# Softmax row maxima taken as minima of scaled scores inside the score pass

## The chip, the core and the metric

The kernel runs on one core of a Trainium2 chip. Its time is the device time of one execution in microseconds (us); the profile shows one execution engine by engine: PE (TensorE matmuls), PEld (its weight loads), DVE (VectorE), ACT (ScalarE), POOL (GpSimd) and SP (which issues most loads).

## What is computed

One decoder layer over 512 tokens of width 1024, in float32. The part that the change touches is the two softmaxes of the attention stage:

```python
# A: sliding window, 8 heads in 4 blocks of 128 queries; a learned sink per head is one more score
scores = where(valid, q @ k * d**-0.5 - slope * delta, -1e30)
probs = softmax(concat([scores, sink]))[..., :-1]
# B: differential attention, 4 heads with two maps each, 4 blocks of 128 queries
scores = where(delta >= 0, q @ k * d**-0.5 - slope * delta, -1e30)
p = softmax(scores)
a = p[:, :, 0] - lam * p[:, :, 1]
```

Around them stand an adaLN-modulated norm, one input projection, gates with their own projections, a merge, an output projection, a second norm, a gated MLP with a width-3 convolution, and a final norm. `slope` is a power of two: 2^-(h+1) for the 8 heads of A, 2^-(2h+2) for the 4 heads of B.

## The kernel before, in words

Every product in float32 accuracy is made of three matmuls on operands split into a high and a low half (`mm3`, L121). The low halves are computed on DVE (L119, L491, L494), the high halves on ACT (L118, L490, L493).

**Order of the work.** In the attention stage only TensorE's order is written by hand. It consists of attention steps and, between them, of *filling* steps: `fill(n)` (L539) runs n steps of the projections that wait in `units`, each step three matmuls of 512 columns. `SWA_FILL` and `DIFF_FILL` say how many stand at each place. DVE, ACT, POOL and SP get their order when the kernel is built, from priorities (`tc.high_priority(offset=HP)` marks the softmax work), a model of each instruction's time, and explicit holds (`tc.issue_after`). Every eighth fill step also starts a piece of the adaLN row products (`ada_rows`, L839: a weight load, then multiplies of 128x512 on DVE, L857 and L859).

**Sliding-window pairs.** Four pairs i of heads h = i + 4j, j = 0, 1. `swa_scores` (L587) makes the scores of a pair in PSUM and then, for each block n and each j, one score pass on DVE (L620): it adds the distance matrix `dsw` to the scores, writes the sum to `sb`, and leaves the row maximum in `mx[:, j, n]`. In the trace it is a CUSTOM_DVE_ANT_0 and a DVE_READ_ACCUMULATOR2_ANT, the readout of the row value. The scores are kept divided by the slope, so that the distance enters with factor 1. `swa_softmax` (L625) turns the maxima of a head into the exponential's bias (L631: minus slope times maximum, and the minimum of that and `nsink`, which is minus the sink), computes the sink's exponential `es` (L632), four exponentials with row sums (L635, scale `slope`), the sum with the sink (L639), its reciprocal (L640), and the normalisation (L644). Then PE transposes the probabilities (`swa_transpose`, L656), ACT copies them out (L658), and `swa_values` multiplies them by v (L666).

**Differential blocks.** s = 4h + n runs over 4 heads and 4 query blocks. `diff_scores` (L716) and `diff_softmax` (L751) take two blocks together: score passes with row maxima for both maps (L744, with the distance matrix `ddf`), maxima times minus slope (L754), exponentials (L764), and on DVE the weight of the second map (L767, L768) and the difference (L769). `diff_transpose` transposes it (L781) and splits it into `aTh` and `aTl` (L490, L491). `diff_values` (L786) multiplies by v into `od`; its statistics (`stats`, L801) and the normalisation by `turn_norm` (L812: transposes `rb`, L815, then `of` times `rb`, L816, and the split into `outd`, L817 by L118 and L119) come later, for the last head at set numbers of fill steps after it.

**The end of the stage** (L998 to L1004): four gate units are added, four fill steps run, the third head's `turn_norm` is flushed, and `diff_values` of the last head runs; after that the fill steps go on until the units are used up. The merge with the differential branch (`pB`, L1044) reads `outd`.

Of the kernel before, what the change touches and what calls it, by code (L numbers as in the profile page):

```python
# [8 lines left out]
F32 = mybir.dt.float32  # L9
F32R = mybir.dt.float32r  # L10
AF = mybir.ActivationFunctionType
ALU = mybir.AluOpType
PSUM = bass.MemoryType.PSUM

P = 128
# [3 lines left out]
NT = S // P  # L19
# [35 lines left out]
def kernel(  # L55
# [22 lines left out]
    nc = tc.nc  # L78
# [3 lines left out]
    def pool(name, bufs=1, space=None, stack=ctx):  # L82
        kw = {} if space is None else {"space": space}
        return stack.enter_context(tc.tile_pool(name=name, bufs=bufs, reuse_waits="tile", **kw))
# [61 lines left out]
    dsw = cpool.tile([P, 256], F32, name="dsw")  # L146
# [3 lines left out]
    ddf = cpool.tile([P, 512], F32, name="ddf")  # L150
# [290 lines left out]
    for gi in range(KT):  # L441
# [4 lines left out]
        else:  # L446
            h_low(gi)
            lp = cpool.tile([P, 2, 64], F32, name="lp")
            ls = cpool.tile([P, 2], F32, name="ls")
# [4 lines left out]
            nsink = cpool.tile([P, 8], F32, name="nsink")  # L454
# [27 lines left out]
    ap = pool("att", stack=at)  # L482
# [51 lines left out]
    def prefetch():  # L534
        while units and len(loaded) < 2:
            load, run = units.pop(0)
            loaded.append((load(), run))

    def fill(n):  # L539
        for _ in range(n):  # L540
            if not current:
                prefetch()
                if loaded:
                    wts, run = loaded.pop(0)
                    current.append(run(wts))
                    if tick[0]:
                        prefetch()
            if tick[0] == 7:
                prefetch()
            if current:  # L550
                try:
                    next(current[0])
                except StopIteration:
                    current.clear()
            for e in list(later):
                e[0] -= 1
                if e[0] <= 0:
                    later.remove(e)
                    e[1]()
            tick[0] += 1  # L560
            if tick[0] >= ADA_START and tick[0] % ADA_EVERY == 0:
                next(ada, None)
# [24 lines left out]
    def swa_scores(i, blocks):  # L587
        if 0 in blocks:
            c = pairs[i] = Pair()
            c.mx, c.nm, c.lsum, c.es = (  # L590
                ap.tile([P, 2, NT], F32, tag=t, bufs=2, name=f"{t}{i}") for t in ("mx", "nm", "lsum", "es")
            )
            c.sb = [ap.tile([P, 2, P], F32, tag="st0", bufs=2, name=f"st{i}_0")]
            c.sb += [ap.tile([P, 2, 256], F32, tag="st", bufs=ST, name=f"st{i}_{n}") for n in range(1, NT)]
            c.pT = []
        c = pairs[i]
        sps = {
            (g, j): vbank(f"sw{i}_{g}_{j}").rearrange("p (a q) -> p a q", a=2)
            if len(blocks) == NT and (g, j) == (1, 1) else sbank(f"sw{i}_{g}_{j}", (P, 2, 256))
            for g in sorted({n // 2 for n in blocks}) for j in range(2)  # L600
        }
        for n in blocks:
            w = P if n == 0 else 2 * P
            k0 = max(0, n - 1) * P
            qs, ks = slice(n * P, (n + 1) * P), slice(k0, k0 + w)
            mm3_rows([
                (
                    sps[n // 2, j][:, n % 2, :w],
                    [qa[64 * j : 64 * j + 64, i, b, qs] for b in range(2)],
                    [ka[64 * j : 64 * j + 64, b, ks] for b in range(2)],  # L610
                )
                for j in range(2)
            ])
        for n in blocks:
            w = P if n == 0 else 2 * P
            if n == 2:
                c.first = c.last
            for j in range(2):
                with tc.high_priority(offset=HP):
                    c.last = nc.vector.tensor_tensor_reduce(  # L620
                        c.sb[n][:, j, :w], sps[n // 2, j][:, n % 2, :w], dsw[:, 256 - w : 256], 1.0, -3e38, ALU.add, ALU.max,
                        c.mx[:, j, n : n + 1],
                    )

    def swa_softmax(i):  # L625
        with tc.high_priority(offset=HP):
            c = pairs[i]
            for j in range(2):
                h = i + 4 * j
                slope = 2.0 ** -(h + 1)  # L630
                nc.vector.tensor_scalar(c.nm[:, j], c.mx[:, j], -slope, nsink[:, h : h + 1], ALU.mult, ALU.min)  # L631
                nc.scalar.activation(c.es[:, j], c.nm[:, j], AF.Exp, bias=sink[:, h : h + 1])  # L632
                for n in range(NT):
                    w = P if n == 0 else 2 * P
                    nc.scalar.activation(  # L635
                        c.sb[n][:, j, :w], c.sb[n][:, j, :w], AF.Exp, bias=c.nm[:, j, n : n + 1], scale=slope,
                        accum_out=c.lsum[:, j, n : n + 1],
                    )
                nc.vector.tensor_add(c.lsum[:, j], c.lsum[:, j], c.es[:, j])  # L639
                nc.vector.reciprocal(c.lsum[:, j], c.lsum[:, j])  # L640
                for n in range(NT):
                    w = P if n == 0 else 2 * P
                    sb = c.sb[n][:, j, :w]
                    c.divided = nc.vector.tensor_scalar_mul(sb, sb, c.lsum[:, j, n : n + 1])  # L644
# [71 lines left out]
    def diff_scores(*ss):  # L716
        ops = []
        for s in ss:
            h, n = divmod(s, NT)
            t = heads[h]  # L720
            w = (n + 1) * P
            if n == 0:
                firsts[h] = [sbank(f"sd{h}_{m}", (P, 2, 256)) for m in range(2)]
            sps = [
                firsts[h][m][:, n, :w] if n < 2 else (vbank if n + m == 4 else sbank)(f"sd{h}_{n}_{m}")[:, :w]
                for m in range(2)
            ]
            mm3_rows([
                (
                    sps[m],  # L730
                    [t[64 * m : 64 * m + 64, b, n * P : (n + 1) * P] for b in range(2)],
                    [t[64 * m : 64 * m + 64, 2 + b, :w] for b in range(2)],
                )
                for m in range(2)
            ])
            ops.append((s, sps, w))
        for s, sps, w in ops:
            h, n = divmod(s, NT)
            mx = ap.tile([P, 2], F32, tag="dmx", bufs=3, name=f"dmx{h}_{n}")
            pm = []  # L740
            for m in range(2):
                st = ap.tile([P, w], F32, tag="st", bufs=ST, name=f"sd{h}_{n}_{m}")
                with tc.high_priority(offset=HP):
                    nc.vector.tensor_tensor_reduce(  # L744
                        st, sps[m], ddf[:, 512 - w : 512], 1.0, -3e38, ALU.add, ALU.max, mx[:, m : m + 1]
                    )
                pm.append(st)
            scored[s] = mx, pm


    def diff_softmax(*ss):  # L751
        with tc.high_priority(offset=HP):
            for s in ss:
                nc.vector.tensor_scalar_mul(scored[s][0], scored[s][0], -(2.0 ** (-2 * (s // NT + 1))))  # L754
            behind = ExitStack()
            for s in ss:
                h, n = divmod(s, NT)
                slope = 2.0 ** (-2 * (h + 1))
                mx, pm = scored[s]
                if n == 0:  # L760
                    sums[h] = ap.tile([P, 2, NT], F32, tag="dls", bufs=2, name=f"dls{h}")
                ls0, ls1 = (sums[h][:, m, n : n + 1] for m in range(2))
                for m, ls in enumerate((ls0, ls1)):
                    exp = nc.scalar.activation(  # L764
                        pm[m], pm[m], AF.Exp, bias=mx[:, m : m + 1], scale=slope, accum_out=ls
                    )
                nc.vector.reciprocal(ls1, ls1)  # L767
                nc.vector.scalar_tensor_tensor(ls1, ls1, ls0, nlam, ALU.mult, ALU.mult)  # L768
                last = nc.vector.scalar_tensor_tensor(pm[0], pm[1], ls1, pm[0], ALU.mult, ALU.add)  # L769
                probs[s] = pm[0]  # L770
                behind.enter_context(tc.issue_after(exp.ins))
                behind.enter_context(tc.issue_after(last.ins))
            behind.close()
# [144 lines left out]
    pairs, firsts, scored, probs, aTs = {}, {}, {}, {}, {}  # L918
# [49 lines left out]
    for s in range(4 * DIFF_HEADS):  # L968
        h, n = divmod(s, NT)
# [27 lines left out]
            fill(DIFF_FILL[3])  # L997
    for j in range(4, KT):  # L998
        add_gate_a(j)
    fill(4)  # L1000
    flush("norm")
    diff_values(DIFF_HEADS - 1)
    while units or loaded or current:
# [220 lines left out]
    st = gpart(3, [P, 2, 4, 256], "s1_t1")  # L1224
# [716 lines left out]
```

## Time and profile before

| | before |
|---|---|
| median of 3 runs | 693.09 us (692.62 to 693.96) |
| the profiled execution | 693.06 us |
| its span, first to last instruction | 691.3 us |
| mean granted TensorE clock | 0.996 |
| sliding-window score passes (L620) | 59.1 to 100.2 us from the span's start |
| differential score passes (L744) | 114.8 to 195.1 us |
| MLP, up projection (L1270) and down projection (L1885) | from 355 and from 579 us |

In the lines of the profile that follow, times are us from the span's start unless marked ns; `out<-in` names the tiles that an instruction writes and reads, then comes the shape (partitions x elements), and `[0.49 <-DVE st L644]` is idle time of the engine before the instruction and what ended it. Matmuls are pipelined, so their durations overlap and the distance of their starts is what one costs. A row of the waits reads: engine, tile, line, released by whom, us in total, times, longest.

### The profile page before, as it was taken

How to read it: one execution, taken by the hardware profiler on the slowest of the kernel's cores; microseconds unless marked ns; L12 is line 12 of the kernel's file. 1: busy time of each engine (PE TensorE's matmuls, PEld its weight loads, DVE VectorE, ACT ScalarE, POOL GpSimd, SP SyncE). 2: the span in 40 equal slices, each digit the busy share in tenths (PEclk: the TensorE clock that was granted, in tenths of full speed). 3: DMA queues.
4: the chain of work that ended last, by engine and by line, in shares of the span. 5: the costliest groups of instructions: out<-in, count | busy, mean ns of one | idle time of the engine just before them, and what ended most of it. 6: DMA issues, size and time to landing. Idle time of an engine off the chain costs nothing. (4 is left out here: it accounts for less than half of the span.)

```text
span 691.3 us, 11249 instructions
## 1 busy us (share of the span) xinstructions
PE 680.5 (98%) x4203; PEld 592.7 (86%) x4203; DVE 565.3 (82%) x1073; ACT 384.6 (56%) x686; POOL 82.1 (12%) x100
## 2 busy tenths in 40 slices
PE   8999999999999999999999999999999999999995
PEld 5787877788888888888889999999999999888884
DVE  5898987987885666663789988888888999979997
ACT  7676666545552323332477756655565666656665
POOL 3000000000001000000030101112111002540300
PEclk9999999999999999999999999999999999999998
DMA  9985454553455675229726798777978748997903
GB/s 307 328 258 165 140 156 151 154 163 96 138 138 169 212 217 180 91 95 315 230 56 129 166 214 197 167 173 215 206 215 217 155 149 207 196 195 199 167 1 121
DMA packets 115926, 121.81 MB, mean 176 GB/s; under 512 B 4447, under 2 KB 93344, under 8 KB 115872
## 3 DMA queue, kind: packets, MB, share of 16 engines
q1 hardware_dynamic: 96958, 95.09, 43.8%
q0 software_dynamic: 18720, 25.73, 22.2%
q8 instruction: 33, 0.54, 0.3%
q10 hardware_dynamic: 194, 0.28, 0.1%
q14 instruction: 21, 0.17, 0.1%
HBM read 118.97 MB, written 2.11 MB: 175 GB/s over the span
## 5 line engine op out<-in xcount | busy, mean ns | idle before, releaser
L1270 PE MATMUL up<-t,m_whi 128*128 128x256 f32 x512 | 93.1, 283 | 0.0
L1270 PEld LDWEIGHTS up<-t,m_whi 128*128 128x128 f32 x512 | 79.9, 192 | 0.0
L1270 PE MATMUL up<-t,m_wlo 128*128 128x256 f32 x256 | 72.4, 283 | 0.0
L1270 PE MATMUL up<-bh,p_whi 128*128 128x256 f32 x232 | 65.7, 283 | 0.0
L1270 PE MATMUL up<-bl,p_whi 128*128 128x256 f32 x232 | 65.7, 283 | 0.0
L1270 PE MATMUL up<-bh,p_wlo 128*128 128x256 f32 x232 | 65.7, 283 | 0.0
L859 DVE SCALAR_TENSOR_TENSOR arow<-ra,cs,arow 128x512 f32<-128x512 f32 x56 | 42.0, 749 | 20.0 <-DMA ra<-in_w_ada_dram 19.4
L1270 PEld LDWEIGHTS up<-t,m_wlo 128*128 128x128 f32 x256 | 49.2, 192 | 0.0
L1270 PEld LDWEIGHTS up<-bh,p_whi 128*128 128x128 f32 x232 | 44.5, 192 | 0.0
L1270 PEld LDWEIGHTS up<-bl,p_whi 128*128 128x128 f32 x232 | 44.5, 192 | 0.0
L1270 PEld LDWEIGHTS up<-bh,p_wlo 128*128 128x128 f32 x232 | 44.5, 192 | 0.0
L1179 POOL DMA_DIRECT2D s<-in_w_up_dram x21 | 27.0, 1361 | 140.8 <-DMA s<-in_w_up_dram 66.5
L1207 ACT CAST m_whi<-s 128x1024 fp32r<-128x1024 f32 x31 | 32.5, 1049 | 11.1 <-DVE s L1201 6.3
L1211 DVE TENSOR_TENSOR m_wlo<-s,m_whi 128x1024 fp32r<-128x1024 f32 x31 | 37.8, 1219 | 0.0
L1270 PE MATMUL up<-t,p_whi 128*128 128x256 f32 x176 | 32.2, 283 | 0.0
L882 POOL DMA_DIRECT2D mod_rows<-row x8 | 4.9, 614 | 204.9 <-ACT row L881 204.9
L1270 PEld LDWEIGHTS up<-t,p_whi 128*128 128x128 f32 x176 | 27.5, 192 | 0.0
L1277 ACT ACTIVATE gT<-a,cv 128x512 f32<-128x512 f32 x22 | 17.8, 816 | 16.9 <-DVE a L1312 15.8
L185 POOL TENSOR_TENSOR r<-ms,mhalf 128x1 f32<-128x1 f32 (+1 forms) x16 | 12.6, 791 | 120.9 <-DVE ms L183 73.1
L1207 ACT CAST p_whi<-wa 128x1024 fp32r<-128x1024 f32 x18 | 18.8, 1046 | 12.5 <-PE up L1270 12.5
L1211 DVE TENSOR_TENSOR p_wlo<-wa,p_whi 128x1024 fp32r<-128x1024 f32 x18 | 22.0, 1223 | 3.8 <-ACT p_whi L1207 3.8
L1270 PE MATMUL up<-t,p_wlo 128*128 128x256 f32 x88 | 24.9, 283 | 0.0
(491 smaller groups left out, 2064.9 us busy)
## 6 DMA issues: line engine op xcount, KB each, us to landing
ra<-in_w_ada_dram SPq DMA_DIRECT2D x32, 512.0 KB, 4.4
wa<-in_w_up_dram SPq DMA_DIRECT2D x22, 512.0 KB, 3.9
s<-in_w_up_dram SPq DMA_DIRECT2D x21, 512.0 KB, 4.5
s<-in_w_up_dram POOLq DMA_DIRECT2D x21, 512.0 KB, 6.6
adaw<-in_w_ada_dram SPq DMA_DIRECT2D x12, 512.0 KB, 7.6
w<-in_w_in_dram SPq DMA_DIRECT2D x12, 512.0 KB, 4.9
a<-in_w_up_dram SPq DMA_DIRECT2D x11, 512.0 KB, 4.5
b<-in_w_down_dram SPq DMA_DIRECT2D x10, 512.0 KB, 4.6
```

The costliest lines, as they stand in the source:

```text
L185: nc.gpsimd.tensor_tensor(r0, ms, mhalf[:, :n], ALU.pow)
L859: nc.vector.scalar_tensor_tensor(ac, r[:, a], cc, ac, ALU.mult, ALU.add)
L882: nc.gpsimd.dma_start(mod_rows[idx, hf * S : (hf + 1) * S].rearrange("(g n) -> g n", g=4), row[0:P:32])
L1179: nc.gpsimd.dma_start(dst, upblock(*blk), accum_op=ALU.add)
L1207: nc.scalar.copy(W[J, name][0], R[J, SRC[name]])
L1211: nc.vector.tensor_sub(lo, R[J, SRC[name]], hi.bitcast(F32))
L1270: nc.tensor.matmul(o[u], w[:, k, cu], b[:, k], start=name in ("p1", "m5", "p2") and k == 0 and x == 0, stop=k == 3 and x == 2, skip_group_ ...
L1277: nc.scalar.activation(grow(j), av[J][:, u], AF.Identity, bias=cv[:, 66 + j : 67 + j], scale=cv[:, 44 + j : 45 + j])
```

## The change

The score pass takes minus the slope as its factor and min as its reduction, so that it writes minus slope times the score and leaves the exponential's bias itself. In the sliding-window part the reduction starts from minus the sink (`nsink`, a column read from memory) instead of from a constant. The instructions that made the bias (L631, L754) and the tile `mx` of the pairs are gone, and the exponentials take scale -1. Beside that the last `fill(4)` of the stage becomes `fill(6)`.

```diff
     def swa_scores(i, blocks):
-            c.mx, c.nm, c.lsum, c.es = (
-                ap.tile([P, 2, NT], F32, tag=t, bufs=2, name=f"{t}{i}") for t in ("mx", "nm", "lsum", "es")
+            c.nm, c.lsum, c.es = (
+                ap.tile([P, 2, NT], F32, tag=t, bufs=2, name=f"{t}{i}") for t in ("nm", "lsum", "es")
             )
...
                     c.last = nc.vector.tensor_tensor_reduce(
-                        c.sb[n][:, j, :w], sps[n // 2, j][:, n % 2, :w], dsw[:, 256 - w : 256], 1.0, -3e38, ALU.add, ALU.max,
-                        c.mx[:, j, n : n + 1],
+                        c.sb[n][:, j, :w], sps[n // 2, j][:, n % 2, :w], dsw[:, 256 - w : 256], -(2.0 ** -(i + 4 * j + 1)),
+                        nsink[:, i + 4 * j : i + 4 * j + 1], ALU.add, ALU.min, c.nm[:, j, n : n + 1],
                     )
...
     def swa_softmax(i):
-                slope = 2.0 ** -(h + 1)
-                nc.vector.tensor_scalar(c.nm[:, j], c.mx[:, j], -slope, nsink[:, h : h + 1], ALU.mult, ALU.min)
                 nc.scalar.activation(c.es[:, j], c.nm[:, j], AF.Exp, bias=sink[:, h : h + 1])
...
-                        c.sb[n][:, j, :w], c.sb[n][:, j, :w], AF.Exp, bias=c.nm[:, j, n : n + 1], scale=slope,
+                        c.sb[n][:, j, :w], c.sb[n][:, j, :w], AF.Exp, bias=c.nm[:, j, n : n + 1], scale=-1.0,
...
     def diff_scores(*ss):
                     nc.vector.tensor_tensor_reduce(
-                        st, sps[m], ddf[:, 512 - w : 512], 1.0, -3e38, ALU.add, ALU.max, mx[:, m : m + 1]
+                        st, sps[m], ddf[:, 512 - w : 512], -(2.0 ** (-2 * (h + 1))), 3e38, ALU.add, ALU.min, mx[:, m : m + 1]
                     )
...
     def diff_softmax(*ss):
-            for s in ss:
-                nc.vector.tensor_scalar_mul(scored[s][0], scored[s][0], -(2.0 ** (-2 * (s // NT + 1))))
...
-                slope = 2.0 ** (-2 * (h + 1))
...
-                        pm[m], pm[m], AF.Exp, bias=mx[:, m : m + 1], scale=slope, accum_out=ls
+                        pm[m], pm[m], AF.Exp, bias=mx[:, m : m + 1], scale=-1.0, accum_out=ls
...
     for j in range(4, KT):
         add_gate_a(j)
-    fill(4)
+    fill(6)
     flush("norm")
     diff_values(DIFF_HEADS - 1)
```

## The prediction

> **What bounds the kernel now.** I read the page first, then the waits of PE, then PE's starts one by one in the attention stage (56 to 245 us), since the change lies there alone. The page has the span, then per engine busy us, share and count.
>
> ```profile
> span 691.3 us, 11249 instructions
> PE 680.5 (98%) x4203; PEld 592.7 (86%) x4203; DVE 565.3 (82%) x1073; ACT 384.6 (56%) x686; POOL 82.1 (12%) x100
> ```
>
> PE is busy for 98% of the span, so at most 691.3 - 680.5 = 10.8 us could be won anywhere by helping another engine. The windows view of 5 us stretches from 50 to 250 us gives the share of this stage; here are the one stretch that matters and the total.
>
> ```profile
> 100.00:105.00 5.00, 4.51 (x23) 3.42 (x23) 3.68 (x14) 4.17 (x19) 0.00 (x0) 1.00 0.67 190
> ...
> sum 200.00, PE 199.13 PEld 159.83 DVE 158.47 ACT 106.12 POOL 10.62; mean PE 4.98 PEld 4.00 DVE 3.96 ACT 2.65 POOL 0.27
> ```
>
> PE is shown idle for 200.00 - 199.13 = 0.87 us of 200, and 0.49 of it lie in this one stretch. The waits of PE say for whom:
>
> ```profile
> PE tp L656 <- DVE st L644: 0.5, 1, 0.5
> PE a L385 <- ACT hThA L369: 0.4, 2, 0.3
> ```
>
> Only the first has to do with a softmax: the transposes of the last sliding-window pair (pair 3) wait for its normalised probabilities. The other belongs to the input projection, as do the rest of that list. So the change can help through the chain that ends in L644, and hardly elsewhere. The timelines of PE, ACT and DVE there (start, duration, engine, line; merged rows carry a count):
>
> ```profile
> 102.77 0.39 PE L123 MATMUL pw<-hTlA,w_h 128*128 128x512 f32 x1
> 102.99 0.39 PE L124 MATMUL pw<-hThA,w_l 128*128 128x512 f32 x1
> 103.88 0.87 PE L656 MATMUL tp<-ident,st 128*128 128x128 f32 x5 [0.49 <-DVE st L644]
> ```
>
> ```profile
> 100.83 0.30 ACT L632 ACTIVATE es<-nm,sink 128x4 f32<-128x4 f32 x1 [2.85 <-DVE nm L631]
> 101.03 0.39 ACT L635 ACTIVATE st<-st,nm 128x128 f32<-128x128 f32 x1
> ...
> 102.80 0.20 ACT L635 ACTIVATION_READ_ACCUMULATOR st<-st,nm 128x1 f32 x1
> ```
>
> ```profile
> 99.81 0.42 DVE L620 CUSTOM_DVE_ANT_0 st<-sw,dsw 128x256 f32<-128x256 f32 x1
> 100.16 0.09 DVE L620 DVE_READ_ACCUMULATOR2_ANT mx<- 128x1 f32 x1
> 100.16 0.42 DVE L620 CUSTOM_DVE_ANT_0 st<-sw,dsw 128x256 f32<-128x256 f32 x1
> 100.50 0.09 DVE L620 DVE_READ_ACCUMULATOR2_ANT mx<- 128x1 f32 x1
> 100.50 0.36 DVE L631 TENSOR_SCALAR nm<-mx,nsink 128x4 f32<-128x4 f32 x2
> 100.77 1.54 DVE L859 SCALAR_TENSOR_TENSOR arow<-ra,cs,arow 128x512 f32<-128x512 f32 x2
> 103.03 0.16 DVE L639 TENSOR_TENSOR lsum<-lsum,es 128x4 f32<-128x4 f32 x1 [0.73 <-ACT st L635]
> 103.23 0.18 DVE L640 RECIPROCAL lsum<-lsum 128x4 f32<-128x4 f32 x1
> 103.44 1.07 DVE L644 TENSOR_SCALAR st<-st,lsum 128x128 f32<-128x128 f32 x4
> ```
>
> Matmuls of 512 columns start 0.22 to 0.23 us apart, so the transposes were due at 102.99 + 0.23 = 103.22 and began at 103.88: PE lost 0.66 us. The chain behind it is score passes on DVE, L631, five activations on ACT, L639, L640, L644, PE. Each step follows the one before at once, except that DVE idles 0.73 us waiting for ACT.
>
> **The removed instructions.** L631 runs 8 times, L754 16 times:
>
> ```profile
> L631 DVE TENSOR_SCALAR nm<-mx,nsink x8: 222/226/229, 63.5 to 100.6; 128x4 f32<-128x4 f32 x8
> ...
>   ACT es L632: 5.4, 4
> ```
>
> ```profile
> L754 DVE TENSOR_SCALAR dmx<-dmx x16: 157/164/172, 115.9 to 196.1; 128x2 f32<-128x2 f32 x16
> ...
>   ACT sd L764: 12.0, 6
> ```
>
> They overlap their neighbours: two L631 took 100.50 to 100.77, 0.135 us each, and of L754 a pair takes less. So DVE is relieved of 8 x 0.135 + 16 x 0.12 = 3.0 us. None of this is path by itself: PE is busy 199.13 of 200 us beside it. What counts is what starts earlier. The "who waited" rows above show ACT standing 5.4 and 12.0 us behind these lines. ACT itself is only 56% busy, so its earlier start is worth something only where PE waits for the end of that softmax.
>
> **Pair 3, head j = 0.** The first L631 ends at 100.50 + 0.23 = 100.73, and ACT's es starts at 100.83: a hop of 0.10. Without L631 es needs the fourth readout of head 0. The passes alternate between the heads, so that is the readout at 100.16, ended at 100.25. es can start at 100.35, **0.48 us earlier**. Behind es on ACT stand four exponentials and their readouts, unchanged in length (only the constant of scale changes), so they all move by 0.48. DVE can follow: its two row products of 1.54 us end before the earlier L639 (now 102.55). L644 then starts at 102.96 and PE's transposes at 103.40. PE still waits 0.18; it wins 0.48 of 0.66. If es had to await the last readout (100.59) instead, it would start at 100.69 and the win is 0.14: the lower end.
>
> **Differential blocks.** Here L754 came behind all four score passes. Without it the first exponential can start after the first readout. In the second pair of blocks:
>
> ```profile
> 123.99 0.08 DVE L744 DVE_READ_ACCUMULATOR2_ANT dmx<- 128x1 f32 x1
> ...
> 126.03 0.23 DVE L754 TENSOR_SCALAR dmx<-dmx 128x2 f32<-128x2 f32 x2
> ...
> 129.58 0.62 DVE L769 SCALAR_TENSOR_TENSOR sd<-sd,dls,sd 128x384 f32<-128x384 f32 x1
> ```
>
> ```profile
> 126.22 0.62 ACT L764 ACTIVATE sd<-sd,dmx 128x384 f32<-128x384 f32 x1 [2.97 <-DVE dmx L754]
> ```
>
> ```profile
> 129.98 0.39 PE L124 MATMUL pA<-outah,wba_l 128*128 128x512 f32 x1
> 130.35 0.52 PE L781 MATMUL td<-ident,sd 128*128 128x128 f32 x3
> ```
>
> The exponential can start at 124.07 + 0.10 = 124.2 instead of 126.22, some 2 us earlier. But PE lost only 130.35 - 129.98 - 0.23 = 0.14 us to this block, and its waits name no other. I take 0.10, with ends 0 and 0.14. So nearly the whole 12.0 us stays hidden behind PE's filling projections.
>
> **What is altered in place.** The score passes get another constant, min for max, and in the sliding-window ones a start value read from memory (nsink, written before this stage on the same engine: no wait is added). No row has such a pass. The nearest rows: L631, which reads nsink, has 226 ns, and a TENSOR_SCALAR of equal shape with constants only is this one:
>
> ```profile
> 202.41 0.17 DVE L181 TENSOR_SCALAR ms<-dr 128x4 f32<-128x4 f32 x1
> ```
>
> So reading the operand costs at most 0.06 us a pass; the lower end is nothing. A separate extra instruction of L631's 0.135 us a pass would be the far end. A gain is excluded: elements and readouts stay. I take nothing, because the pass is long beside its operand. The Trainium skill ("VectorE: DVE Perf Modes", Two Vector instructions with no wait between them) says that a pointer scalar makes the next Vector instruction wait only where it starts in another quadrant of partitions than another input; by it the price is nothing, since all tiles here start at partition 0. No run here shows it yet.
>
> **fill(6) for fill(4).** Two more filling steps of three matmuls (2 x 3 x 0.23 = 1.4 us) go ahead of the broadcast transposes rb of head 2 and the values od of head 3. PE's sum is the same.
>
> ```profile
> 207.66 0.68 DVE L491 TENSOR_TENSOR aTl<-td,aTh 128x512 fp32r<-128x512 f32 x1
> ```
>
> ```profile
> 208.21 0.48 PE L122 MATMUL od<-aTh,qkv 128*128 128x512 f32 x1
> 208.53 0.39 PE L123 MATMUL od<-aTl,qkv 128*128 128x512 f32 x1
> ```
>
> The second od matmul comes 0.19 us after aTl is ready (208.34). With PE 0.58 earlier and DVE at its old time it would wait up to 0.39; the two steps cover that with 1.0 to spare. What they push back is the last head's output, last written at 233.0:
>
> ```profile
> L123 PE MATMUL pB<-outdB,wbd x32: 389/389/389, 253.9 to 308.8; 128*128 128x512 f32 x32
> L119 DVE TENSOR_TENSOR outdB<-of,outdA x4: 685/690/693, 163.8 to 233.0; 128x512 fp32r<-128x512 f32 x4
> ```
>
> It ends at 233.0 + 0.69 + 1.4 = 235.1 instead; the first reader is at 253.9. The moved block issues no DMA. The two steps themselves come earlier, ahead of rb and od, and with them any weight load on SP's queue that they let start; that gives a load more time, not less. Cost: nothing.
>
> **Sum.** 0.48 + 0.10 = 0.58 us off the profiled execution, whose own time is 693.06 us (span 691.3 and 1.76 around it; the median of the runs is 693.09): **692.5**. Behind this stage PE stays the bound, so the gain should arrive at the end. Bounds: 0.14 + 0 gives 692.9; 0.66 + 0.14, all that PE lost here, gives 692.3.
>
> **Rivals.** *Slower: DVE's order.* Only TensorE's order is written by hand in this stage; DVE, ACT and SP are ordered when the kernel is built, by priorities and a model of time. With 24 instructions fewer, another piece of work can fall in front of a softmax that PE needs soon. Place: the gap before L639. The row products would run from 100.59 to 102.13, so DVE has 102.55 - 102.13 = 0.42 us free there. One more row product (1.54 / 2 = 0.77) makes the transposes 0.35 later than in the forecast; the low half of a weight, the longest filler, makes them 0.80 later:
>
> ```profile
> 95.62 1.22 DVE L119 TENSOR_TENSOR wga_l<-wga,wga_h 128x1024 fp32r<-128x1024 f32 x1
> ```
>
> So it costs from 0.42 us on, and turns the gain into a loss from 0.42 + 0.48 = 0.90 on. At the td of 130.35, which has no slack in the old order, the same fillers cost their whole 0.77 to 1.22. One place gives 692.9 to 693.7, both with the long filler 692.5 + 0.80 + 1.22 = 694.5, and more places more; that is the time of this rival, 694.5 to 696. For it: 24 softmax chains (8 heads, 16 blocks) with fillers between, and two places without slack. Against: softmax work has the highest priority.
>
> *Slower, by the pass.* With the far end, 7 passes x 0.135 = 0.95 ahead of the readout, less 0.48: the transposes 0.47 later than before, 693.5. It decides from 0.48 / 7 = 0.07 us a pass; the 0.06 above gives 0.42, a win of 0.06 left.
>
> *No effect:* ACT is given es only behind all passes (692.9, the lower end above), or starts it where it did (693.1).
>
> *Faster by more.* The weight loader stands idle with no cause shown ahead of changed steps:
>
> ```profile
> PEld sd L129 <- issue: 2.2, 8, 0.4
> PEld td L781 <- issue: 1.5, 4, 0.4
> ```
>
> Twelve such switches, about 0.1 us of PE each (208.53 - 208.21 is 0.32 where 0.23 is usual). Were they late signals from the softmax, the earlier ACT would end them: 692.5 - 1.2 = 691.3. Against: the same pause stands where operands have long been there.
>
> **How the numbers follow.** Forecast 692.5: 0.48. No effect: 0.12. DVE's order: 0.28, of which 0.22 over 694.5, since several places would go together. Pass price: 0.04. Faster by more: 0.08. A difference within 0.2% (1.39 us, 691.7 to 694.5) is about what a measurement of this kernel can tell from no change. So faster 0.08, same 0.70, slower 0.22. The range, 691.6 to 695.5, leaves out about half of the chance of either outer case, 0.15 in all. The forecast's own range is 692.2 to 692.9.
>
> **What would show it.** L631 and L754 gone and DVE busy near 562.3; score passes at 420 ns for 256 columns; es of pair 3 at 100.35 and PE's wait for L644 near 0 to 0.2 us; the first exponential of a differential pair some 2 us earlier with PE's starts unmoved but for 0.6 us; od without a wait. Wrong would make it: passes over 0.49 us, a new PE wait that names a DVE line, or another order of fillers ahead of L639 or L769.

## The result, and the profile after

The changed kernel takes **697.5 us** (median; 695.08 to 700.81), the kernel before 692.86 us beside it on the same chip (691.81 to 694.06): ratio 1.0063, 95% interval 1.0044 to 1.0082. By the ratio it is slower by 4.4 us, 0.63%, above the forecast and above its range. (All ratios below are against the kernel before, run beside each experiment on the same chip.) The profiled execution took 695.33 us and so lies near the fast end; its losses are the smaller ones. From `swa_softmax` on, a line of the changed kernel has the number of before less 2, behind `diff_softmax` less 5: `L644` is now `L642`, `L912` is `L907`, `L859` is `L854`.

The page of the changed kernel: its span, and busy us, share and count of each engine.

```profile
span 693.6 us, 11230 instructions
PE 680.8 (98%) x4203; PEld 592.7 (85%) x4203; DVE 562.6 (81%) x1049; ACT 383.3 (55%) x686; POOL 82.0 (12%) x100
```

DVE lost its 24 instructions and is busy 562.6 us, 562.3 were forecast (a match by luck, as the section on the prediction shows). PE does the same work. So PE stood idle, and the waits of PE in the changed kernel say for whom:

```profile
PE tp L654 <- DVE st L642: 1.1, 1, 1.1
PE pgd L122 <- DVE ta L907: 0.9, 1, 0.9
PE pA L122 <- DVE ta L907: 0.7, 1, 0.7
PE od L123 <- DVE aTl L491: 0.4, 1, 0.4
PE td L776 <- DVE qkv L491: 0.2, 1, 0.2
```

Of these only tp was there before, with 0.5; pgd lies behind 250 us, the others before. The windows view of 50 us stretches from 50 to 250 us ends in this row for the changed kernel:

```profile
sum 200.00, PE 197.21 PEld 157.77 DVE 152.51 ACT 103.27 POOL 10.57; mean PE 49.30 PEld 39.44 DVE 38.13 ACT 25.82 POOL 2.64
```

PE is idle for 2.79 us of these 200, against 0.87 before. The loss lies in this stage: from its first scores (sw) to the first pB the kernel before takes 195.5 us (58.1 to 253.6) and the changed kernel 198.9 (57.2 to 256.1), and from there to the end they take 437.7 and 437.5. DVE is busy for 6.0 us less in the stage but only for 2.7 less in all: some of its work slid behind the stage. So DVE idled more, and was late more. The waits of DVE name a suspect, the first row before, the second after:

```profile
DVE arow L859 <- DMA ra<-in_w_ada_dram: 19.4, 15, 2.9
```

```profile
DVE arow L854 <- DMA ra<-in_w_ada_dram: 35.2, 16, 7.3
```

These are the row products (arow), each of which multiplies a block of a weight that has just been loaded into ra. Not all of the difference costs time: the kernel before with fill(6) alone (e4 below) loses nothing and has this row, with nearly the same longest wait.

```profile
DVE arow L859 <- DMA ra<-in_w_ada_dram: 26.2, 16, 6.9
```

Here is a stretch of DVE before, then the same stretch after (start, duration, engine, line):

```profile
126.16 0.74 DVE L859 SCALAR_TENSOR_TENSOR arow<-ra,cs,arow 128x512 f32<-128x512 f32 x1
126.82 0.68 DVE L912 SCALAR_TENSOR_TENSOR ta<-ta,pA 128x512 f32<-128x512 f32 x1
127.88 0.75 DVE L859 SCALAR_TENSOR_TENSOR arow<-ra,cs,arow 128x512 f32<-128x512 f32 x1 [0.38 <-DMA ra<-in_w_ada_dram]
```

```profile
125.91 0.73 DVE L854 SCALAR_TENSOR_TENSOR arow<-ra,cs,arow 128x512 f32<-128x512 f32 x1
...
127.18 0.75 DVE L854 SCALAR_TENSOR_TENSOR arow<-ra,cs,arow 128x512 f32<-128x512 f32 x1 [0.41 <-DMA ra<-in_w_ada_dram]
127.85 0.61 DVE L764 SCALAR_TENSOR_TENSOR sd<-sd,dls,sd 128x384 f32<-128x384 f32 x1
...
128.45 0.73 DVE L854 SCALAR_TENSOR_TENSOR arow<-ra,cs,arow 128x512 f32<-128x512 f32 x1
...
129.23 0.68 DVE L907 SCALAR_TENSOR_TENSOR ta<-ta,pA 128x512 f32<-128x512 f32 x1
```

Nobody edited the order of these five. Before, ta ran at 126.82, ahead of a product whose load had not landed. Now two more products and a softmax step stand ahead of it, and it runs at 129.23. PE's next pA waits for it:

```profile
129.97 0.50 PE L122 MATMUL pA<-outah,wba_h 128*128 128x512 f32 x1 [0.69 <-DVE ta L907]
```

The longest wait for a load, again DVE of the changed kernel:

```profile
236.58 0.75 DVE L854 SCALAR_TENSOR_TENSOR arow<-ra,cs,arow 128x512 f32<-128x512 f32 x1 [7.29 <-DMA ra<-in_w_ada_dram]
237.25 0.68 DVE L811 TENSOR_TENSOR of<-of,rb 128x512 f32<-128x512 f32 x1
```

The product stands for 7.29 us at DVE's head, and all that is queued behind it stands too. PE waits for nothing until the pgd at 250.47, though, and the 6.9 us in e4 cost nothing. So the sum of DVE's waits is not the price; what counts is what is queued behind a wait and how soon PE needs it.

At pair 3 the changed passes are seen, and in the same kernel a differential pass, whose start value is a constant, at another time:

```profile
99.68 0.48 DVE L620 CUSTOM_DVE_ANT_0 st<-sw,dsw,nsink 128x256 f32<-128x256 f32 x1
100.08 0.08 DVE L620 DVE_READ_ACCUMULATOR2_ANT nm<- 128x1 f32 x1
```

```profile
157.64 0.42 DVE L742 CUSTOM_DVE_ANT_0 sd<-sd,ddf 128x256 f32<-128x256 f32 x1
```

A pass that reads its start value from memory takes 0.48 us in place of 0.42; one with a constant keeps 0.42, although its operation was changed to a minimum too.

### The profile page after: what moved, and what is told of

It reads as the page before. It is cut to its first block, busy times and chain, and to the rows that moved or that the text cites. A ratio compares the mean times of both kernels' runs of the same rounds, so it can differ in the third digit from the quotient of the medians.

```text
span 693.6 us, 11230 instructions
## 1 busy us (share of the span) xinstructions
PE 680.8 (98%) x4203; PEld 592.7 (85%) x4203; DVE 562.6 (81%) x1049; ACT 383.3 (55%) x686; POOL 82.0 (12%) x100
## 4 chain that ended last, share of the span: by engine, by line
PE 76%; DVE 11%; DMA 9%; issue 2%; ACT 1%; POOL 0%; SPq 0%; POOLq 0%; DVEq 0%; ACTq 0%
PE up L1265 32%; PE dc L1880 15%; DMA ra<-in_w_ada_dram 8%; PE a L385 5%; DVE arow L854 3%; PE oc L1321 2%; PE oc L1322 2%; PE oc L1325 2%; PE pgd L122 2%; PE pgd L124 2%; PE pgd L123 2%; DVE st L620 1%; PE pB L122 1%; PE pB L123 1%; PE pB L124 1%
## 5 line engine op out<-in xcount | busy, mean ns | idle before, releaser
L854 DVE SCALAR_TENSOR_TENSOR arow<-ra,cs,arow 128x512 f32<-128x512 f32 x56 | 41.9, 747 | 35.8 <-DMA ra<-in_w_ada_dram 35.2
L759 ACT ACTIVATE sd<-sd,dmx 128x128 f32<-128x128 f32 (+3 forms) x32 | 17.7, 555 | 20.3 <-DVE dmx L742 20.3
```

The costliest lines, as they stand in the source:

```text
L759: exp = nc.scalar.activation(pm[m], pm[m], AF.Exp, bias=mx[:, m : m + 1], scale=-1.0, accum_out=ls)
L854: nc.vector.scalar_tensor_tensor(ac, r[:, a], cc, ac, ALU.mult, ALU.add)
```

## The experiments

Theory: the change by itself costs nothing, but DVE and ACT are ordered anew when the kernel is built, and in the new order something that PE needs comes late. Rivals: the slower passes, and the moved filling steps. TensorE's order is the same in all kernels below, but for the place of the two filling steps.

**Old order, new order.** In e1, e2 and several later ones the order of DVE and ACT is held by edges that order instructions without a wait:

```diff
+    def pin(engine, order):
+        cur = nc.cur_bb.bb.instructions
+        mine = [i for i in cur if i.engine == engine]
+        dep = mybir.DependencyInfo(mybir.DependencyClass.NoSync, mybir.DependencyReason.DATA)
+        for p, q in zip(order, order[1:]):
+            tc.add_manual_dep(mine[q], mine[p].name, dep, reason="pin")
```

e1 is the change with fill(4), both engines in the order of before:

> The change with fill(4), with the instructions of DVE and ACT held in the exact order that they have in the kernel before (edges that fix the order of issue only; the 24 removed instructions are simply missing). Theory 'order': the loss comes from the new order that the planner gave DVE and ACT, so this one is not slower than before: 692 to 693.2 against 692.9, with no wait of PE over 0.7 us in the attention stage. Rival 'passes': the sliding-window passes, 420 ns before and 480 ns in the changed kernel, are the cause, so it stays slow, 695 to 698. Rival 'fill': with fill(4) it should be fast whatever the order, so this run alone cannot tell it from 'order'; the third and fourth run do.

Measured: 692.66 us, ratio 1.0002 (0.9988 to 1.0016). Its waits of PE in the stage are the one row of before:

```profile
PE tp L654 <- DVE st L642: 0.5, 1, 0.5
```

e2 is the reverse, the instructions of before in the order of the changed kernel:

> The kernel before, with all its instructions, its constants and fill(4), but DVE and ACT held in the order of the changed kernel (with fill(4)); the bias instructions stand right behind the passes that they need. Theory 'order': slow like the changed kernel, 695 to 699, with the waits for row products, ta and transposes that the changed kernel shows. Rival 'passes' or 'fill': within 0.3% of before, 692 to 694.5.

Measured: 703.05 us, ratio 1.0141 (1.0122 to 1.0160), with PE waiting 2.0 us at the first pA for ta. The order alone is enough for a loss, and the change alone is worth nothing that can be measured. But e2 loses more than twice what the changed kernel does and lies above the 695 to 699 expected; all of it lies in the stage (205.5 us from the first scores to the first pB, 195.5 before). Why the old instructions fare worse in the new order was not followed.

**The filling steps.** e3 is the change with fill(4), e4 the kernel before with fill(6); nothing is held.

```diff
-    fill(6)
+    fill(4)
```

> The change with fill(4) left as it was, nothing held. Theory 'order': still slow, 695 to 700, since fill(6) is not the cause; the values of the last head wait for aTl a little more than in the changed kernel (0.5 to 2 us). Rival 'fill': back at 692 to 693.5.

> The kernel before with fill(6) for fill(4) alone. Theory 'order': within 0.2% of before, 692 to 694, as the order of DVE changes only at the end of the stage. Rival 'fill': 695 or more.

Measured: e3 697.53 us, ratio 1.0062 (1.0047 to 1.0078); e4 692.84 us, 1.0002 (0.9992 to 1.0012). The filling steps cost nothing. In e3 PE waits longer for aTl at od:

```profile
PE od L123 <- DVE aTl L491: 1.4, 1, 1.4
```

With fill(6) it was 0.4. So the two steps do cover od, for about 1 us; the whole doesn't show it.

**Which half brings the order.** e5 has the sliding-window half of the change alone (the edits at L591, L621 to 622, L631 and L635), e6 the differential half alone (L745, L754, L764); both with fill(4), nothing held.

> Only the sliding-window half of the change (8 instructions fewer, passes with the sink as start value), differential blocks as before, fill(4), nothing held. In its order the product ta (L912) of the first pA stays ahead of the second-last row products near 126 us, as before. Theory (the differential half brings the bad order): 692.4 to 693.3, ratio 0.9995 to 1.0005, and no wait of PE for ta over 0.3 us; passes of 128x256 at 0.48 us; wait of the transposes tp 0.5 to 1.2 us. Rival (any re-planning costs the same, or the passes do): 695 to 698.

> Only the differential half of the change (16 instructions fewer), sliding-window part as before, fill(4), nothing held. In its order two row products, one of which waits for its load, stand ahead of the product ta near 126 us. Theory (this half brings the bad order): 695 to 698, PE waiting 0.7 to 1.6 us for ta. Rival (the sliding-window half brings it): 692.5 to 693.3 without that wait.

Measured: e5 692.99 us, 1.0007 (0.9994 to 1.0021), no wait for ta; e6 695.10 us, 1.0037 (1.0022 to 1.0052), with these rows first among its waits of PE:

```profile
PE pA L122 <- DVE ta L909: 1.5, 1, 1.5
PE od L123 <- DVE aTl L491: 1.4, 1, 1.4
```

So the 32 slower passes alone are harmless, and the differential half is not. It makes 0.37% of the 0.62% of e3; the rest comes only with both halves (e3 waits 1.2 us at tp, e6 not at all). e12 asks what about the 16 removed multiplications matters. It is the whole change with fill(4), with an idle step in their place that the exponentials read:

```diff
     def diff_softmax(*ss):
         with tc.high_priority(offset=HP):
+            for s in ss:
+                idle = ap.tile([P, 2], F32, tag="didle", bufs=3, name=f"didle{s}")
+                nc.vector.tensor_scalar_mul(idle, scored[s][0], 1.0)
+                scored[s] = idle, scored[s][1]
```

> The whole change with fill(4), nothing held, but in the differential softmax a multiplication by one of the bias columns (128x2, 16 times) stands where the removed one stood, and the exponentials read its result. The two engines' orders come back close to those of the sliding-window part alone. Theory (the removed dependence, not the passes or the constants, let the order go astray): 692.4 to 693.4, no wait for ta, tp wait 0.5 to 1. Rival (the new passes or constants cost): 695 to 697.5.

Measured: 692.58 us, 1.0002 (0.9990 to 1.0013), no wait for ta. An instruction that computes nothing takes the ratio from 1.0062 (e3) to 1.0002. The exponentials depended on a step on DVE; without it they are ready sooner, and the order is planned anew. That it is this dependence, and not just any other list of instructions, is argued: an idle step at another place was not run.

**One engine alone.** e7 holds DVE in the old order and ACT in the new, e9 the reverse.

> The whole change with fill(4); VectorE's instructions held in the order of before, ScalarE's in the order that the changed kernel gave itself. Theory (what PE waits for stands late in VectorE's order): 692.4 to 693.4, PE waits tp 0.5 to 0.7 and nothing else over 0.4. Rival (ScalarE's order, exponentials ahead of the copies PE needs): 695 to 698.

> The whole change with fill(4); VectorE held in the order that the changed kernel gave itself, ScalarE in the order of before. The counterpart of e7. Theory (the two orders only fit as a pair; at a mismatch one engine's head waits for what stands far down the other's queue): slower than before, 695 to 701, with PE waits that name VectorE lines other than in the changed kernel. Rival (ScalarE's order alone carries the loss, as e7 can be read): 692.4 to 693.5, PE waits as before.

Measured: e7 698.93 us, 1.0089 (1.0072 to 1.0105); e9 701.71 us, 1.0137 (1.0116 to 1.0157). My theory for e7, that VectorE's order alone decides, is wrong; e9 lies a little above the 695 to 701 expected. e7's waits of PE begin with a row that the changed kernel doesn't have:

```profile
PE td L776 <- DVE dls L762: 4.3, 3, 2.0
```

The timelines of ACT and DVE in e7 show why:

```profile
160.22 1.04 ACT L118 CAST w_h<-w 128x1024 fp32r<-128x1024 f32 x1
```

```profile
161.29 1.23 DVE L119 TENSOR_TENSOR w_l<-w,w_h 128x1024 fp32r<-128x1024 f32 x1 [2.99 <-ACT w_h L118]
162.43 0.68 DVE L491 TENSOR_TENSOR aTl<-td,aTh 128x512 fp32r<-128x512 f32 x1
163.03 0.15 DVE L762 RECIPROCAL dls<-dls 128x1 f32<-128x1 f32 x1
```

ACT in its new order does the exponentials first and then w_h. DVE in its old order has w_l ahead of the softmax and stands 2.99 us for it. The two orders belong together; each with the other's partner is slower than the changed kernel, e9 clearly, e7 with an interval that touches that of e3.

**One place.** e8 is the new order on both engines, with only the eight ta put back behind their neighbours of before. Only one of them moves far, by six places: the one that the first pA waits for.

> The whole change with fill(4), both engines held in the order that the changed kernel gave itself, but the 8 products ta of VectorE put back to their places of before (behind the same neighbour): ahead of the row products near 126 us. Theory A (one place makes most of the loss, and the rest follows from it): 693 to 694. Theory B (each place costs its own wait, about 1 us each): the wait for ta near 129 goes and 1 to 1.5 us with it, 696 to 696.7. Rival (ta does not matter): 697.5.

Measured: 695.02 us, 1.0043 (1.0023 to 1.0062), against 1.0062 for e3: 0.19%, 1.3 us less, though the intervals overlap. The wait for ta is gone, and PE still waits 1.9 us at tp and 1.4 at od. That fits theory B in the ratio (its time came out lower, as before ran 0.6 us quicker beside these runs than beside e3), each place with a cost of its own, but does not prove it.

**Why the order costs.** In e10 and e11 the products read a resident tile, so that they never wait for a load; the product with the loaded weight is left out. e10 has the new order, e11 the old.

```diff
-                        nc.vector.tensor_scalar_mul(ac, r[:, a], cc)
+                        nc.vector.tensor_scalar_mul(ac, hT[0][0], cc)
...
-                        nc.vector.scalar_tensor_tensor(ac, r[:, a], cc, ac, ALU.mult, ALU.add)
+                        nc.vector.scalar_tensor_tensor(ac, hT[0][a], cc, ac, ALU.mult, ALU.add)
```

> The whole change with fill(4), both engines held in the order of the changed kernel; the row products of the condition vector read a resident tile instead of the block just loaded, so that they never wait for a load; the loads themselves stay. It leaves out the product with the loaded weight. Theory A (the new order costs because products that wait for their load stand ahead of what PE needs): the wait for ta near 129 us under 0.3, total 692.5 to 694.5. Rival B (the order costs by the length of the work ahead alone): 696 to 697.5. Row products 0.75 us each in both.

> Control for e10: the same kernel without waits for those loads, both engines held in the order of before. 691.5 to 692.8 under either theory, since in the old order PE waited for none of these products; the wait of the transposes tp near 0.6 us stays.

Measured: e10 690.92 us (690.70 to 691.58), 0.9972 (0.9961 to 0.9983); e11 690.74 us (690.66 to 691.03), 0.9970 (0.9958 to 0.9982). Without those waits the two orders take the same time, both less than before and less than expected. The windows from 50 to 250 us of e10 end in this row:

```profile
sum 200.00, PE 200.00 PEld 161.40 DVE 159.57 ACT 104.45 POOL 10.60; mean PE 50.00 PEld 40.35 DVE 39.89 ACT 26.11 POOL 2.65
```

PE is never idle. I had expected tp's 0.6 us to stay in e11, and it went too: so the chain of pair 3 had begun with a load. Before, DVE had stood here just ahead of the passes of pair 3:

```profile
94.95 0.75 DVE L859 SCALAR_TENSOR_TENSOR arow<-ra,cs,arow 128x512 f32<-128x512 f32 x1 [1.64 <-DMA ra<-in_w_ada_dram]
95.62 1.22 DVE L119 TENSOR_TENSOR wga_l<-wga,wga_h 128x1024 fp32r<-128x1024 f32 x1
96.75 0.69 DVE L494 SCALAR_TENSOR_TENSOR qkv<-pq,qkv 128x512 fp32r<-128x512 f32 x1
97.36 0.28 DVE L620 CUSTOM_DVE_ANT_0 st<-sw,dsw 128x128 f32<-128x128 f32 x1
```

e10 takes away two things, the waits and the readers that keep the loads' buffers. e13 is e10 with a late reader for the buffers:

```diff
+                if before is not None:
+                    seen = wp.tile([P, 1], F32, tag="seen", bufs=2, name=f"seen{idx}{hf}_{k}")
+                    nc.vector.tensor_copy(seen, before[:, 0, 0:1])
...
-            r = nxt
+            before, r = r, nxt
```

> As e10 (new order, row products read a resident tile, which leaves out the product with the loaded weight), but each loaded block is read by a 128x1 copy on VectorE behind the last product of the next block, so that its buffer comes free one period later than in the changed kernel, while the reader hardly ever waits. Theory A (products waiting at VectorE's head): 690.7 to 692.5, no wait for ta. Rival B (buffers freed late shift the later loads): 694 to 698, with loads that start later than in e10.

Measured: 696.88 us, 1.0063 (1.0049 to 1.0078), which by the total would be for the buffers. But its windows from 50 to 250 us say otherwise:

```profile
sum 200.00, PE 200.00 PEld 161.73 DVE 161.08 ACT 105.57 POOL 10.59; mean PE 50.00 PEld 40.43 DVE 40.27 ACT 26.39 POOL 2.65
```

PE is never idle here either, in spite of buffers that are held longer. That they are held shows in the loads: those at 192.27 and 225.33 in e10 start at 200.07 and 232.03 here, later by far more than the 1.6 us by which e13 comes to the stage late. From the first scores to the first pB e13 takes 194.1 us, e10 194.3. Of the 6.0 us between their spans 1.6 lie ahead of the stage (first scores at 58.6 and 57.0) and 4.6 behind it (442.2 and 437.6 us from the first pB on), in matmuls that became longer (ns min/median/max), e10 first:

```profile
L122 PE MATMUL pB<-outdA,wbd x32: 389/389/398, 251.3 to 306.2; 128*128 128x512 f32 x32
```

```profile
L122 PE MATMUL pB<-outdA,wbd x32: 393/394/398, 252.7 to 308.4; 128*128 128x512 f32 x32
```

Within the stage they are equal (389 for pga in both). So buffers held late, with the loads that they delay, cost the stage nothing as long as no product waits for a load; why later matmuls are 5 ns longer in e13 is open (the one thing that I see reaching there is a small tile more in the weights' pool, and I did not try another place for it).

**The remedy.** e14 (new order) and e15 (old order) keep the whole computation and load each block two steps ahead of its products instead of one:

```diff
-        r = ada_load(*todo[0])
+        ring = [ada_load(*job) for job in todo[:2]]
...
-        for (idx, hf, k), job in zip(todo, todo[1:] + [None]):
-            nxt = ada_load(*job) if job else None
+        for (idx, hf, k), job in zip(todo, todo[2:] + [None, None]):
+            r = ring.pop(0)
+            if job:
+                ring.append(ada_load(*job))
```

> The whole change with fill(4), both engines held in the order of the changed kernel, nothing left out; each row block is loaded two steps ahead of its products instead of one (one buffer of four more is taken). Theory A: products wait less for loads (under 12 us in all instead of 24 to 35), 691 to 694. Rival B (buffers): loads of weights are pushed back, 695 to 700.

> As e14 with both engines held in the order of before. Theory A: 690.7 to 692.7, at or below before, since the 1.8 us that e11 gained came from the missing waits. Rival B: 694 to 699.

Measured: e14 691.60 us, 0.9990 (0.9981 to 0.9999); e15 690.76 us, 0.9977 (0.9967 to 0.9986). The order that cost 0.62% in e3 costs nothing against before now, and in the old order this version beats both kernels. DVE's waits for these loads, and PE at the transposes of pair 3, both in e15:

```profile
DVE arow L856 <- DMA ra<-in_w_ada_dram: 5.4, 4, 2.5
```

```profile
101.78 0.40 PE L124 MATMUL pw<-hThA,w_l 128*128 128x512 f32 x1
102.02 0.93 PE L654 MATMUL tp<-ident,st 128*128 128x128 f32 x7
```

The transposes follow the projection after 0.24 us: no wait is left. e16 to e18 ask for remedies with nothing held. e16 is the change with fill(4) and no raised priority for the products; e17 is the kernel before, e18 the changed kernel with fill(6), both with the loads two steps ahead.

```diff
-                hold = tc.high_priority(offset=HP // 2)
+                hold = ExitStack()
```

> The whole change with fill(4), nothing held, row products without raised priority, so that the planner may put ta and the softmax in front of them. Theory A: if ta comes ahead of the products near 126 us and products wait less, 692 to 695; no wait of PE for ta. Rival: the products come too late and the row's end is waited for, over 697.

> Kernel before, fill(4), nothing held, each row block loaded two steps ahead of its products. Theory (products waiting at VectorE's head are what makes the orders differ in time): 690.5 to 691.7, no wait of PE over 0.3 us in the attention stage but tp. Rival (planner spoils it): 692.5 to 695.

> The changed kernel as it is, fill(6), nothing held, each row block loaded two steps ahead of its products. Theory: within 0.1% of e17, 690.3 to 691.8, the loss of the change gone. Rival (the re-planned order costs by itself): 694 to 697.

Measured: e16 693.37 us, 1.0015 (1.0004 to 1.0027); e17 693.87 us, 1.0019 (1.0008 to 1.0029); e18 692.35 us, 0.9993 (0.9984 to 1.0002). e16 takes back most of the loss, and PE waits for no ta in it. e17 and e18 missed what was expected, e18 by 0.6 us. In e17 the planner, given other load times, chose yet another order, in which PE waits elsewhere:

```profile
PE td L781 <- DVE dls L767: 1.5, 2, 0.8
```

Nor did the earlier loads shorten DVE's waits where nothing is held; e17's row is this, with the 19.4 us of before:

```profile
DVE arow L861 <- DMA ra<-in_w_ada_dram: 19.4, 10, 3.9
```

With the loads ahead it is the changed kernel that is quicker, by 1.5 us (0.22%): the sign is turned round. What decides each time is the order that the planner finds, and how much of DVE's waiting stands ahead of what PE needs.

## Why the prediction was wrong

**The step that failed** is the one under the sum: that behind the removed instructions everything keeps its place and only moves earlier. The order of DVE and ACT did not stay (e1 against e3: 4.9 us). The prediction had this as its rival "DVE's order", with the chance 0.28 and 694.5 to 696. Kind and sign were right, and so was one of its two places, the gap ahead of L639 (now L637). There a third row product now stands behind the passes of pair 3, and the last two start after a wait for their load:

```profile
100.08 0.75 DVE L854 SCALAR_TENSOR_TENSOR arow<-ra,cs,arow 128x512 f32<-128x512 f32 x1
101.13 1.54 DVE L854 SCALAR_TENSOR_TENSOR arow<-ra,cs,arow 128x512 f32<-128x512 f32 x2 [0.30 <-DMA ra<-in_w_ada_dram]
102.59 0.15 DVE L637 TENSOR_TENSOR lsum<-lsum,es 128x4 f32<-128x4 f32 x1
```

ACT was done for L637 at 102.01, so the products make it some 0.55 us late; tp was due at 102.19 and began at 103.43, 1.24 us lost in place of 0.66. The other place, the td at 130.35, did not come true; the ta ahead of pA came in its stead. At od and pgd the lost time was in no new neighbour: just ahead of aTl at od stand the same ta and wga_l as before, and ahead of pgd's ta the same steps as in e4. DVE as a whole came late there, because products further up waited longer for their loads. On the way to od the two below wait 1.34 and 1.40 us, where the same two waited 0 and 0.50 before:

```profile
196.79 0.49 DVE L852 TENSOR_SCALAR arow<-ra,cs 128x512 f32<-128x512 f32 x1 [1.34 <-DMA ra<-in_w_ada_dram]
203.33 1.54 DVE L854 SCALAR_TENSOR_TENSOR arow<-ra,cs,arow 128x512 f32<-128x512 f32 x2 [1.40 <-DMA ra<-in_w_ada_dram]
```

The load for the second is itself late with DVE: SP starts it at 199.58, just after a product ends (198.82 + 0.73 = 199.55); before, it started at 196.96, just after one that ended at 196.93. So, as far as these times show, a late product delays the next load through its buffer, and that load the next product.

The rival priced a filler at its own length, 0.77 to 1.22 us. What it left out is the time that a product at DVE's head still waits for its load; e10, e14 and e15 show that without most of these waits the new order costs nothing. The reason against the rival, that softmax work has the highest priority, does not bear: at pA it was ta and the products that had changed places.

**What bounds the kernel now.** PE at 98% is right, but the chain behind the 0.66 us of tp was read back only to the score passes, "each step follows the one before at once". Three rows further up stood a product with 1.64 us of waiting. The list of DVE's waits had 19.4 us for the same load, and the prediction made no use of it, since no PE wait named it.

**DVE's relief** of 3.0 us was read too high: a pair of L754 took 126.16 - 126.03 = 0.13 us, 0.07 each and not 0.12, which makes 2.1 in all, and the 32 longer passes take 1.9 back. That DVE came to 562.6 us is luck: in e1, with the same instructions in the old order, it is busy 564.6.

**Pair 3.** Its es did lose the step, and got it back as longer passes. In e1, which has the old order, the product ahead of the passes starts at 94.28 and ACT's es at:

```profile
100.09 0.30 ACT L630 ACTIVATE es<-nm,sink 128x4 f32<-128x4 f32 x1 [2.87 <-DVE nm L620]
```

That is 5.81 us behind it; before it was 100.83 - 94.95 = 5.88. The win is 0.07 in place of 0.48, and PE's wait stays at 0.5.

**The pass price** was the mis-sized term: nothing was taken, 0.06 us was the upper row bound, and 0.06 was measured (0.42 to 0.48; 7 passes make 0.42, "a win of 0.06 left" as the rival had it). The readout behind starts 0.08 us before the pass ends, 0.07 to 0.08 before, so nothing stands between the two, and there the trace agrees with the Trainium skill ("VectorE: DVE Perf Modes", Two Vector instructions with no wait between them). But I had read from that rule that the pass has no price, and the pass itself grew. The measurement decides. It costs no time by e5.

**Differential blocks.** Right: the first exponential of the block pair starts at 123.90 instead of 126.22, 2.3 us earlier (2.1 when counted from the first pass) where 2.0 were expected, and PE gains nothing from it:

```profile
123.90 0.62 ACT L759 ACTIVATE sd<-sd,dmx 128x384 f32<-128x384 f32 x1 [3.23 <-DVE dmx L742]
```

That it can start earlier goes, by e6 and e12, with the new order of the rest.

**fill(6)** costs nothing, as forecast (e4), and covers od in part. It did not give the loads more time, though: in e4 the longest wait for one is 6.9 us, 2.9 before. The 1.0 us to spare was not enough, since the last aTl was ready at 210.92 in the changed kernel where 208.34 was reckoned with, 2.58 us later. The ta and the wga_l of 1.22 us just ahead of it stood there before too; what was late is the product at 203.33 above, 2.56 us behind its time of before:

```profile
210.24 0.68 DVE L491 TENSOR_TENSOR aTl<-td,aTh 128x512 fp32r<-128x512 f32 x1
```

**No effect** is what the change is in the old order (e1), but not for the rival's reasons: es did start behind the fourth readout of its own head, and the longer passes ate what that gave. **Faster by more** showed in no kernel that loads as before.

**What is open.** How the planner gets from earlier exponentials to products ahead of ta was not followed step by step, nor was e13's later slowdown. The share of a single place in the 4.4 us was tried for ta alone (e8, about 1.3 us, not parted from none by its interval).

## What to carry to other kernels

Where engines are ordered when the kernel is built, removing a step that hides behind other work can cost more than it saves, because the plan of everything else moves; look at the order of the changed build before believing a sum of local gains. An instruction that waits for a load at the head of an in-order engine is the weak point: list what is queued behind each such wait, also where today no bound engine waits for it, and issue that load earlier. Here that helped with the order held (e14, e15); with nothing held the plan moved again (e17). Holding the old order by edges separates what a change does from what its plan does.

## What the runs showed of the hardware

A score pass whose start value is read from memory takes 0.06 us longer than one with a constant, at 128x256 (0.42 to 0.48) and at 128x128 (0.28 to 0.34). The times of e3, in which PE waits behind products that wait for loads, spread over 4.2 us in 6 runs, those of e10, the same order without these waits, over 0.9 us in 6 runs; but e1, with 0.5 us of such waiting, spreads over 4.5 us in 12 runs, so the waits are not shown to be the reason. And a wait can hide in another engine's list: 19.4 us of DVE's waiting before, with 0.5 us of PE's, was worth 2.0 us by the medians (e11 690.74 against 692.69, e15 690.76 against 692.78). In the stage itself the traces show 1.3 of it (194.2 us in both from the first scores to the first pB, 195.5 before).
